# One gate tile moved from the indexer into the top-k selection, more matmul work a selection round, and a second buffer for the keys read back from DRAM

## The chip, the cores and the metric

The kernel runs on one core of a Trainium2 chip. The metric is the device time of one execution in microseconds (us), lower is better. Engines: PE is TensorE, which does all matrix products and transposes; DVE is VectorE; ACT is ScalarE; POOL is GpSimd; SP is SyncE, which here only issues DMA transfers. Each engine runs its own queue of instructions in order. An instruction that has to wait holds up all that is queued behind it.

## The reference

One inference step of one layer of a streaming encoder: a prompt of 1024 rows and a sample of 32 rows (T = 1024, TS = 32, NT = 1056 rows in all) with D_MODEL = 1024. What the change touches is this part (shapes for the prompt):

```
z = h @ w_in                    # columns: u, zs, q, k, v, za, qi, ki, wi, gm
logits = einsum('bthd,bsd->bths', qi, ki_all) * IDX_DIM ** -0.5   # 8 indexer heads of 64
score = einsum('bth,bths->bts', wi, relu(logits))                 # (1024, 1024), causal by chunks
top_val, top_idx = lax.top_k(score, n_sel)                        # 256 keys for a query, 136 for the sample
s = einsum('bthd,btkhd->bthk', q, kg) * HEAD_DIM ** -0.5          # attention over the chosen keys
merged = sigmoid(g_s) * (ys @ w_ps) + sigmoid(g_a) * (ya @ w_pa)  # g_s, g_a = the 2048 columns gm
```

The 2048 columns gm make 16 gate tiles of 128 columns. A gate tile is a product of h with 128 columns of w_in, a tanh, and a store to DRAM. It needs nothing but h and is read only much later, in the merge, so it may be done at any time before.

## The kernel before, in words

**Numbers.** Every matrix product with w_in is made of three passes in split fp32: weights wh + wl and activations hH + hL, `mm3` (L270), whose three matmuls stand on L271, L272 and L273. `wparts` (L253) makes wh (a rounded copy, L259 on ACT or L263 on POOL) and wl (a subtraction, L264 on DVE or POOL) of a raw tile of weights that L250 loads by DMA.

**The stream.** All products with w_in are jobs of a queue `Z` (class `Stream`, L574), each 128 output columns wide. A job has 8 steps over the contraction for each of three blocks of 256, 384 and 416 rows (`BW`), one `mm3` a step: 72 matmuls. Near its start, a job lets the next job's weights be split and those of the one after it be loaded (`ahead`, L600). At the end of a block, a function of the job takes the result out of PSUM: for a gate tile a tanh on ACT (`tg`, L707), and after the third block the store thD on SP (L709). The program doesn't run the queue in one go: `run(us)` (L652) emits steps worth so many us, by a cost written into the code (0.02 + 0.00132 times the block's rows a step: 0.36, 0.53 and 0.57 us, 11.6 us for a job). PE's order is the order in which the program is written (`manual_schedule`, L715), so these calls set what stands where on PE. In the selection and attention, DVE and ACT have the written order too (L1600); elsewhere, and on POOL and SP everywhere here, a scheduler chooses it.

**The indexer** (L1178 to L1235). The four indexer query tiles qi0 to qi3, two heads each, are stream jobs. For each pair of heads there is a loop over seven row tiles (`i` = 2 to 8; 8 is the sample) and two heads: two passes of products into `pss` (L1220, L1221), relu on ACT (`rl`, L1223), weighting and accumulation in the score tile on DVE (`sco`, L1226, L1228). After every such item, `run(0.25 + nk * FI)` puts a step of stream work on PE. `pss` and `rl` have two buffers each. The first products need `kiL`, which POOL makes (L77). Which jobs can be taken is set by `NI`:

```
Z.add(qijob(1), *(gate_job(f, se, ve) for f in range(NS, NI - 1)))            # L1135
Z.add(qijob(2), qijob(3), gate_job(NI - 1, se, ve), hold=True)                # L1136
```

With NS = 6 and NI = 8, gate tile 6 comes behind qi1 and is taken before and during the first pair's loop; qi2 fills the second pair's loop, qi3 the third's, gate tile 7 the fourth's. ACT and DVE split these tiles' weights (`se, ve`).

**The selection** (L1605 to L1661) finds the threshold of the 256th (136th) score of each row bit by bit in 32 rounds. A round counts, for seven score tiles, the keys that pass the trial threshold: four tiles on ACT (L1556), three on DVE (L1558, 1024, 896 and 640 keys). Then DVE compares the counts (`keep`, L1614) and makes the next threshold (`thr`, L1621), for which the counts of the next round wait. Between the counts and `keep` stands `run(RS)`: stream work of RS = 4.1 us a round. Whatever this emits for ACT or DVE (the blocks' way out of PSUM) thus stands at that place of their queues. The way out is emitted `LAG` = 4.5 us of stream cost after its block. After the rounds, `mark` (L1623) makes the masks `mb` for the seven tiles, mainly on DVE, with `run` calls worth 45 us of stream cost. Stream jobs here: K, V and Q of the first pair of attention heads, gate tiles 8 to 15 and the four tiles za0 to za3; POOL splits the weights (for za1 to za3, ACT makes wh). All jobs must have been emitted before attention begins (`Z.until("za3")`, L1663). While the selection runs, PSUM holds six blocks of stream results: two tiles with two blocks each (`pss`) and two with one (`pz`).

**The keys' way through DRAM.** The K job's result `zf` is stored (L1337), and read back by head into both halves of a tile `kd` of 128 x 512 (`khead`, L1273; two DMAs a load, L1281; two loads a head), from which DVE makes `kH` (L76) and DVE or POOL `kL` (L77). The cached keys `ckt` (L1342), which PE transposes (L1348), use the same buffer: tag "kd", one buffer.

**Attention** (L1689) has 4 x 17 items, each with products (`pss`, L1392), row minima of the negated scores with the mask added (L1398), exponentials (L1405), a transpose two items later (`turn`, L1485) and the product with the values three items later (`pspo`, L1502, L1504), with stream work between: the next pair's K, V, Q and later the products `m0` to `m7`. The merge and the output product follow.

## Time and profile before

| | us |
|---|---|
| median of 3 runs (1029.61 to 1031.7) | 1030.85 |
| the profiled execution | 1031.07 |
| its span, first to last instruction | 1029.3 |
| up to the indexer's first product | 308.5 |
| indexer, to the first K matmul of the selection | 79.0 |
| selection, to the last mask | 196.8 |
| attention, about to 870 | 285.7 |
| merge and output | 159.3 |

An instruction's row in the trace gives start, duration, engine, line, operation, result and operands, and in brackets the idle time before it and what ended it. Durations of matmuls overlap, since they are pipelined; their pace is read from the starts. The row of a stretch gives busy time and the number of instructions of each engine, then the clock granted to TensorE as a share of full speed.

### The profile page before, as it was taken

Reading aid. Unit: us, or ns where it says so; the run is one execution under the profiler, and the core shown is the slowest. Engines: PE = TensorE matmul, PEld = TensorE weight load, DVE = VectorE, ACT = ScalarE, POOL = GpSimd, SP = SyncE. Lnnn points to the kernel's source line nnn. Section 1 sums busy time; section 2 is a strip of 40 time slices with the busy share of each in tenths; the row PEclk is TensorE's granted clock in tenths of the full one; section 3 lists DMA queues with packets and bytes.
Section 4 is the critical chain, followed back from the end, with each engine's and each line's share of the span. In section 5 each row is a group of like instructions: output and inputs, shape, how many; then the busy total and the mean of one; then the engine's idle time right before and its main releaser. Section 6 shows DMA issues by size and latency. Waiting matters only on the chain.

```text
span 1029.3 us, 16904 instructions
## 1 busy us (share of the span) xinstructions
PE 974.4 (95%) x6034; PEld 904.5 (88%) x6034; DVE 762.7 (74%) x1743; ACT 526.5 (51%) x1126; POOL 233.4 (23%) x443
## 2 busy tenths in 40 slices
PE   5999999999999999989998999999999998999997
PEld 3789999999998889889998999999997997998786
DVE  4669899993866879899999758657557685886543
ACT  3642234435546666867994366466465554343111
POOL 3102400000010043333315423334311222530000
PEclk9999999999999999989998999999999999999999
DMA  9922524548483122323313422222416424653411
GB/s 318 277 78 84 147 74 120 128 98 260 134 260 103 40 83 83 93 65 106 102 63 105 136 85 63 88 79 63 132 56 205 131 64 151 209 171 118 133 62 61
DMA packets 134399, 124.24 MB, mean 121 GB/s; under 512 B 20400, under 2 KB 115076, under 8 KB 134316
## 3 DMA queue, kind: packets, MB, share of 16 engines
q1 hardware_dynamic: 133376, 122.62, 38.9%
q8 instruction: 47, 0.77, 0.3%
q10 hardware_dynamic: 780, 0.52, 0.2%
q14 instruction: 36, 0.29, 0.1%
q0 software_dynamic: 160, 0.03, 0.0%
HBM read 87.74 MB, written 34.83 MB: 119 GB/s over the span
## 4 chain that ended last, share of the span: by engine, by line
PE 70%; ACT 9%; DVE 8%; DMA 6%; issue 5%; POOL 1%; SPq 1%; POOLq 0%; ACTq 0%; DVEq 0%
PE pz L271 12%; PE pz L272 11%; PE pz L273 11%; ACT junkb L1556 5%; PE pss L1392 3%; PE psm L1891 3%; PE psm L1892 3%; PE psm L1893 3%; DMA wm<-in_w_mod 2%; PE pt L1485 2%; DVE junk L1558 2%; PE pspo L1504 2%; PE pss L271 2%; PE pss L273 2%; PE pss L272 2%
## 5 line engine op out<-in xcount | busy, mean ns | idle before, releaser
L271 PE MATMUL pz<-hH,wh 128*128 128x384 f32 (+4 forms) x760 | 259.9, 342 | 0.8 <-ACT tg L707 0.5
L272 PE MATMUL pz<-hL,wh 128*128 128x384 f32 (+4 forms) x760 | 250.4, 329 | 0.0
L273 PE MATMUL pz<-hH,wl 128*128 128x384 f32 (+4 forms) x760 | 250.3, 329 | 0.0
L264 POOL TENSOR_TENSOR wl<-raw,wh 128x256 fp32r<-128x256 f32 (+1 forms) x180 | 134.5, 777 | 105.5 <-ACT wh L259 105.2
L271 PEld LDWEIGHTS pz<-hH,wh 128*128 128x128 f32 (+1 forms) x760 | 143.1, 188 | 7.1 <-issue 3.0
L272 PEld LDWEIGHTS pz<-hL,wh 128*128 128x128 f32 (+1 forms) x760 | 142.5, 187 | 1.7
L273 PEld LDWEIGHTS pz<-hH,wl 128*128 128x128 f32 (+1 forms) x760 | 142.1, 187 | 1.3
L1556 ACT ACTIVATE junkb<-sco,thr 128x768 bf16<-128x768 f32 (+3 forms) x128 | 96.7, 756 | 32.0 <-DVE thr L1621 21.2
L1558 DVE TENSOR_SCALAR_CACHE_REDUCE junk<-sco,thr 128x1024 bf16<-128x1024 f32 (+2 forms) x96 | 105.4, 1098 | 2.2
L271 PE MATMUL pss<-hH,wh 128*128 128x256 f32 (+2 forms) x288 | 94.9, 329 | 7.7 <-POOL wl L264 4.1
L273 PE MATMUL pss<-hH,wl 128*128 128x256 f32 (+2 forms) x288 | 92.5, 321 | 2.4 <-POOL wl L264 2.4
L272 PE MATMUL pss<-hL,wh 128*128 128x256 f32 (+2 forms) x288 | 92.5, 321 | 0.0
L1488 DVE TENSOR_TENSOR PL<-pt,PH 128x512 fp32r<-128x512 f32 (+2 forms) x96 | 50.4, 552 | 34.4 <-ACT PH L1487 34.2
L263 POOL CAST wh<-raw 128x256 fp32r<-128x256 f32 x88 | 34.9, 437 | 175.7 <-PE pz L272 157.1
L271 PEld LDWEIGHTS pss<-hH,wh 128*128 128x128 f32 x288 | 57.3, 199 | 11.8 <-POOL wl L264 4.4
L1487 ACT CAST PH<-pt 128x512 fp32r<-128x512 f32 (+2 forms) x96 | 43.0, 483 | 46.4 <-PE pt L1485 45.2
L273 PEld LDWEIGHTS pss<-hH,wl 128*128 128x128 f32 x288 | 57.1, 198 | 3.1 <-POOL wl L264 3.1
L1228 DVE SCALAR_TENSOR_TENSOR sco<-rl,wi,sco 128x384 f32<-128x384 f32 (+6 forms) x49 | 46.9, 964 | 15.0 <-ACT rl L1223 13.9
L272 PEld LDWEIGHTS pss<-hL,wh 128*128 128x128 f32 x288 | 57.2, 199 | 0.3 <-DVE hL L77 0.2
L1223 ACT ACTIVATE rl<-pss 128x384 f32<-128x384 f32 (+6 forms) x56 | 40.9, 739 | 28.0 <-PE pss L1221 22.2
L1405 ACT ACTIVATE Sm<-Sm,mx 128x128 f32<-128x128 f32 (+8 forms) x68 | 52.7, 775 | 4.8 <-DVE mx L1398 4.4
L1893 PE MATMUL psm<-o,mL 128*128 128x512 f32 (+1 forms) x136 | 51.8, 381 | 0.0
(400 smaller groups left out, 2173.9 us busy)
## 6 DMA issues: line engine op xcount, KB each, us to landing
raw<-in_w_in SPq DMA_DIRECT2D x44, 512.0 KB
thD<-tg SPq DMA_DIRECT2D x16, 528.0 KB
tgl<-thD SPq DMA_DIRECT2D x16, 528.0 KB
wm<-in_w_mod SPq DMA_DIRECT2D x8, 1024.0 KB
rraw<-in_w_mod SPq DMA_DIRECT2D x4, 1024.0 KB
kd<-kd SPq DMA_DIRECT2D x32, 128.0 KB
xo<-in_x_prompt SPq DMA_DIRECT2D x8, 512.0 KB
rawo<-in_w_o SPq DMA_DIRECT2D x8, 512.0 KB
```

Of the source, the lines that this page charges most:

```text
L264: leng.tensor_sub(wl[:, c], raw[:, c], f32(wh[:, c]))
L271: te.matmul(ps, wh, xh, start=first, stop=False)
L272: te.matmul(ps, wh, xl, start=False, stop=False)
L273: te.matmul(ps, wl, xh, start=False, stop=last)
L1223: se.activation(rl[:m, :nk].rearrange("p (b c) -> p b c", c=w_), pv, AF.Relu)
L1228: ve.scalar_tensor_tensor(sco[i][:m, :nk], rl[:m, :nk], w, sco[i][:m, :nk], op0=ALU.mult, op1=ALU.add)
L1405: se.activation(P, P, AF.Exp, scale=-1.0, bias=self.mx, accum_out=self.rs)
L1487: se.copy(PH[:, b0:b1_, oc], src)
L1488: ve.tensor_sub(PL[:, b0:b1_, oc], src, f32(PH[:, b0:b1_, oc]))
L1556: se.activation(junkb[:m, :nk], x[:m], AF.Sign, bias=t, accum_out=cnt[:m, k:k + 1])
L1558: ve.tensor_scalar(junk[:m, :nk], x[:m], t, None, op0=ALU.is_lt, op1=ALU.add, accum_out=cnt[:m, k:k + 1])
L1893: te.matmul(ps, ml, wh, start=False, stop=last)
```

## The change

Three numbers of the code are changed, and two places use the last of them:

```diff
-NS, NI = 6, 8
+NS, NI = 6, 7
-LAG, RS, MS, RM, RB = 4.5, 4.1, 0.008, 14.0, 1
+LAG, RS, MS, RM, RB = 4.5, 4.6, 0.008, 14.0, 1
         def load(b):
             c = slice(512 * b, 512 * b + 512)
-            kd = ap_.tile([128, 512], F32, name="kd", bufs=1)
+            kd = ap_.tile([128, 512], F32, name="kd", bufs=2)
             for hf_ in range(2):
                 sp.dma_start(kd[64 * hf_:64 * hf_ + 64], X.kd[64 * e:64 * e + 64, c])
...
             def fin_():
-                ckt = ap_.tile([128, 4, 128], F32, name="ckt", tag="kd", bufs=1)
+                ckt = ap_.tile([128, 4, 128], F32, name="ckt", tag="kd", bufs=2)
```

With NI = 7 the list on L1135 holds no gate tile, and gate tile 6 takes the place of tile 7 on L1136. Tile 7 becomes the first of nine gate tiles in the selection, `gate_job(f, ge, ge) for f in range(NI, 16)` (L1571), and POOL splits its weights. RS = 4.6 puts 32 x 0.5 = 16 us more of stream cost into the 32 rounds.

On PE, the queue loses the gate tile's matmuls before and inside the first pair's loop. Before, the loop's start (`pss` are the indexer's products, `pz` the gate tile's):

```order
L1220 MATMUL pss<-kiH,qis_2929 128x384
L1221 MATMUL pss<-kiL,qis_2929 128x384
L271 MATMUL pz<-hH_738,wh 128x416
L272 MATMUL pz<-hL_739,wh 128x416
L273 MATMUL pz<-hH_738,wl 128x416
L1220 MATMUL pss<-kiH,qis_2930 128x384
L1221 MATMUL pss<-kiL,qis_2930 128x384
```

and with the change, from the transposes ahead of the loop (`pg` is a small product for the output gate):

```order
L1185 MATMUL pt<-idf,cki 128x128 x4
L1194 MATMUL pt<-idf,zki 128x72 x8
L1194 MATMUL pt<-idf,zki 32x72
L1167 MATMUL pg<-rraw,scP 32x512 x4
L1220 MATMUL pss<-kiH,qis_2929 128x384
L1221 MATMUL pss<-kiL,qis_2929 128x384
L1220 MATMUL pss<-kiH,qis_2930 128x384
L1221 MATMUL pss<-kiL,qis_2930 128x384
```

The 72 matmuls of one job are gone from there, 24 of them from inside the loop, and stand in the selection.

On ACT, the blocks leave PSUM earlier, counted in rounds. At the end of the rounds (L1556 are the counts of one round, `tg` a gate block, `wh` the weights of za1, L1629 the first instruction of the marks) before:

```order
L707 ACTIVATE tg<-pss 128x384
L259 CAST wh<-raw 128x1024
L1629 ACTIVATE junkb,cnt<-le 128x1024
L707 ACTIVATE tg<-pz 128x416
L696 ACTIVATE zt<-pss 128x256
```

and with the change, where `wh` stands a round earlier and the last gate block and the first block of za0 (`zt`) ahead of the marks:

```order
L259 CAST wh<-raw 128x1024
L1556 ACTIVATE junkb,cnt<-sco_3313,thr 128x768
L1556 ACTIVATE junkb,cnt<-sco_3311,thr 128x512
L1556 ACTIVATE junkb,cnt<-sco_3310,thr 128x384
L1556 ACTIVATE junkb,cnt<-sco_3316,thr 32x544
L707 ACTIVATE tg<-pz 128x416
L696 ACTIVATE zt<-pss 128x256
L1629 ACTIVATE junkb,cnt<-le 128x1024
```

Before, the 24 gate blocks of the selection leave from round 10 on (rounds counted from 0); with the change, 27 of them from round 9 on.

On SP, the reads of the keys move. In the selection, from the store of the first K result on, before:

```order
L1337 DMA kd_4423<-zf 128x1024
L1267 DMA out_k_p<-tm 128x8x128
L250 DMA raw<-in_w_in 128x8x128
L1268 DMA out_k_s<-tm 32x128
L1281 DMA kd<-kd_4423 64x512 x2
L1267 DMA out_v_p<-tm 128x8x128
L250 DMA raw<-in_w_in 128x8x128
```

and with the change:

```order
L1337 DMA kd_4337<-zf 128x1024
L1281 DMA kd<-kd_4337 64x512 x2
L1267 DMA out_k_p<-tm 128x8x128
L1268 DMA out_k_s<-tm 32x128
L250 DMA raw<-in_w_in 128x8x128
L1281 DMA kd<-kd_4337 64x512 x2
L1267 DMA out_v_p<-tm 128x8x128
```

The first read stands right behind the store, and a load of weights (L250) has moved behind one more store.

## The prediction

> **What bounds the kernel now.** I read the page first, then stretches of the span, then who waits for whom in the two stages that the change touches, and last single rows. On the page, the busy time of the engines and their share of the span:
>
> ```profile
> PE 974.4 (95%) x6034; PEld 904.5 (88%) x6034; DVE 762.7 (74%) x1743; ACT 526.5 (51%) x1126; POOL 233.4 (23%) x443
> ```
>
> PE is short of 100% by 55 us. The change takes no matmul away, so it can only gain from this idle time and from time at a lower clock. Where these lie, the stretches show: the rounds up to the attention heads' last keys, the rest of the rounds, and the marks. The columns are length, busy time (instructions) of PE, PEld, DVE, ACT and POOL, and the granted clock.
>
> ```profile
> 396.30:450.60 54.30, 52.09 (x326) 50.26 (x324) 48.17 (x104) 41.59 (x101) 17.22 (x34) 1.00 0.29 84
> 450.60:541.90 91.30, 84.10 (x505) 82.25 (x504) 85.14 (x196) 79.02 (x191) 26.00 (x48) 0.96 0.28 88
> 541.90:584.30 42.40, 39.10 (x226) 38.34 (x227) 40.70 (x58) 17.03 (x39) 20.93 (x23) 0.92 0.35 114
> ```
>
> Here DVE is as full as PE. The pace is that of the rounds, as the rows of `thr` show, which end a round each (start, duration):
>
> ```profile
> 404.88 0.17 DVE L1621 SCALAR_TENSOR_TENSOR thr<-keep,nxt 128x7 int32<-128x7 int32 x1
> 408.87 0.17 DVE L1621 SCALAR_TENSOR_TENSOR thr<-keep,nxt 128x7 int32<-128x7 int32 x1
> 413.04 0.67 DVE L1621 SCALAR_TENSOR_TENSOR thr<-keep,nxt 128x7 int32<-128x7 int32 x1
> 444.51 0.17 DVE L1621 SCALAR_TENSOR_TENSOR thr<-keep,nxt 128x7 int32<-128x7 int32 x1
> 496.20 0.66 DVE L1621 SCALAR_TENSOR_TENSOR thr<-keep,nxt 128x7 int32<-128x7 int32 x1
> 541.73 0.17 DVE L1621 SCALAR_TENSOR_TENSOR thr<-keep,nxt 128x7 int32<-128x7 int32 x1
> ```
>
> A bare round takes 408.87 - 404.88 = 3.99 us. The last eleven take (541.73 - 496.20) / 11 = 4.14. The rounds with the heads' extra work are longer: from 413.04 (round 4) to 444.51 (round 9) five take 31.5 us. PE waits for these rounds, because a block's way out of PSUM stands on ACT behind them:
>
> ```profile
> PE pss L271 <- POOL wl L264: 4.1, 1, 4.1
> PE pss L273 <- POOL wl L264: 2.4, 2, 1.7
> PE pt L1261 <- ACT tm L1263: 2.2, 2, 2.0
> PE pss L271 <- ACT tg L707: 1.6, 2, 0.8
> PE pss L271 <- ACT wh L259: 1.2, 1, 1.2
> PE pss L271 <- POOL wh L263: 0.7, 1, 0.7
> PE pz L271 <- ACT tg L707: 0.5, 1, 0.5
> ```
>
> This is PE from 387 to 585 us, in all 12.7 us. The longest wait is put down to POOL, but just before it ended ACT took the block of 384 columns out of the `pss` tile that PE needed, behind the counts of round 11; its row and that of the wait follow. What the wait cost beyond its 4.05 us, two stretches of one block each show (24 matmuls of 256 columns):
>
> ```profile
> 454.09 0.46 ACT L707 ACTIVATE tg<-pss 128x384 f32<-128x384 f32 x1
> ```
> ```profile
> 454.69 0.55 PE L271 MATMUL pss<-hH,wh 128*128 128x256 f32 x1 [4.05 <-POOL wl L264]
> ```
> ```profile
> 411.51:414.23 2.72, 2.72 (x25) 2.72 (x24) 2.50 (x7) 2.24 (x7) 2.68 (x6) 1.00 0.03 9
> 454.69:459.95 5.26, 5.26 (x24) 5.26 (x25) 5.02 (x15) 3.87 (x10) 0.01 (x1) 0.50 0.05 18
> ```
>
> After the wait the clock is 0.50, and the block takes 5.26 us instead of 2.72. So the selection is bound by DVE's and ACT's rounds, and PE stands idle at their side; and a wait of 4 us on PE costs 2.5 more behind it.
>
> **The change part by part.** *The indexer loses a job.* One stream job is 72 matmuls; one such stretch, then the rows at the first pair's loop (POOL makes `kiL`; PE's first product; PE's first stream matmul behind the loop), the loop's stretch, and the relus in it (ACT alone):
>
> ```profile
> 438.93:450.50 11.57, 11.57 (x73) 11.34 (x72) 10.37 (x21) 4.59 (x11) 4.44 (x9) 1.00 0.18 47
> ```
> ```profile
> 304.07 3.56 POOL L77 TENSOR_TENSOR kiL<-kid,kiH 128x1568 fp32r<-128x1568 f32 x1 [12.71 <-DVE kiH L76]
> 308.50 0.34 PE L1220 MATMUL pss<-kiH,qis 128*128 128x384 f32 x1
> 323.63 0.33 PE L271 MATMUL pz<-hH,wh 128*128 128x384 f32 x1
> ```
> ```profile
> 308.50:323.60 15.10, 13.80 (x73) 12.07 (x73) 9.61 (x13) 11.06 (x16) 0.00 (x0) 1.00 0.41 137
> ```
> ```profile
> 308.50:323.60 15.10, 9.43 (x13) 1.00 0.41 137
> ```
>
> So 11.57 us of PE work leave this place, but not 11.57 us of time. The first product can't start before `kiL` is there, at 304.07 + 3.56 = 307.6 instead of 308.5. The loop is then bound by its 14 relus, 14 x 9.43 / 13 = 10.2 us, with about 0.5 of a first product ahead: 10.7 us at full clock. But PE will have been idle for most of 300 to 307.6, and as after the wait at 454.69 I expect half clock for some 5.3 us, which costs 2.6 us of PE work; the relus hide a part, I take 2.0. PE leaves the loop at 307.6 + 12.7 = 320.3 instead of 323.6: **3.3 us earlier**. The bounds: full clock all along, 5.3 earlier; half clock all along, where PE's own work in the loop (15.1 less 1.3 idle, less the gate tile's block of 416 of 1056 columns, 4.6, so 9.2) doubles to 18.5, which is 2.5 later. Behind it nothing changes: gate tile 6 fills the fourth loop as tile 7 did, so the 3.3 us arrive at the selection.
>
> *The selection gains a job.* First DVE's side. Its work up to the last mask is the same, less a wait for the keys:
>
> ```profile
> DVE kH L76 <- DMA kd<-kd: 1.0, 1, 1.0
> ```
>
> The second buffer lets this read start early: -1.0 us. Against it stands POOL, which now splits tile 7: in the row of 413.04 `thr` took 0.67 instead of 0.17 beside POOL's work; `keep` and the next `nxt` stand at the same place, so one more job costs up to 3 x 0.5 = 1.5, and I take 1.0, so that the two cancel. Three more blocks on ACT in the rounds lie in the 0.15 us that 4.14 exceeds 3.99 by. The last mask:
>
> ```profile
> 583.86 0.43 DVE L1637 TENSOR_TENSOR mb<-le,eq 32x544 bf16<-32x544 bf16 x1
> 586.14 0.31 DVE L1414 TENSOR_SCALAR Sm<-Sm,rs 128x128 f32<-128x128 f32 x1
> ```
>
> It ends at 584.3 now, so at 581.0, and the first attention item is ready for its transpose 2.2 us later, at 583.2.
>
> A rule of the Trainium skill speaks against this part: "SBUF — State Buffer", section "Who interferes with whom", says that VectorE and GpSimd share a pair of ports under an exclusive lock, and that the loser waits for a whole instruction. The row of 413.04 agrees in kind. Taken at its worst, DVE would stand for the whole 4.4 us of POOL's work on a job (an estimate, from the stretch of 438.93); the masks would then end 3.4 us later than I say, the transpose would be ready at 586.6 and not 584.9 (below), and the time would be 1.7 us longer, 1026.6.
>
> *PE's side.* From the first K matmul to the first attention product, and the first transpose of attention:
>
> ```profile
> 387.55 0.38 PE L271 MATMUL pss<-hH,wh 128*128 128x256 f32 x1
> 583.18 0.22 PE L1392 MATMUL pss<-kH,qs 128*128 128x128 f32 x1
> 589.91 0.27 PE L1485 MATMUL pt<-idf,Sm 128*128 128x128 f32 x1
> ```
>
> 583.18 - 387.55 = 195.6 us. Off go 12.7 of waits, 2.6 at half clock (0.5 x 5.26) and 8% of the 42.4 us of the marks at clock 0.92, 3.4: 176.9 of work. With one job more it is 188.5. With RS = 4.6 a round holds 4.6 x 11.57 / 11.6 = 4.6 us of PE work, so blocks leave PSUM in earlier rounds (order on ACT above), and the waits for them shrink. I keep the 2.2 for `tm`, which the slow rounds cause, and of the other 10.5 about 2.3 (the weights of za1 still pass ACT, then POOL), with 1.0 at half clock. So 384.25 + 188.5 + 5.5 = 578.2 us for the end of the stream. PE then has 589.91 - 583.18 = 6.7 us to do ahead of the first transpose, which needs no mask: 584.9, later than DVE's 583.2. The first transpose stands at 584.9 instead of 589.9: **5.0 us earlier**. The bounds: if half of the 10.5 and half of the 6.0 lost to the clock stay, the stream ends at 384.25 + 188.5 + 2.2 + 5.3 + 3.0 = 583.2 as now, and nothing is gained here; if all go, DVE's 583.2 sets the transpose, 6.7 earlier.
>
> *Attention.* PE waits here for the cached keys, twice:
>
> ```profile
> PE pt L1348 <- DMA ckt<-in_cache_k: 2.6, 2, 1.7
> ```
>
> With its own buffer `ckt` can be read before the last keys are used. But on SP, the reads now wait right behind the store of the keys, and weights behind them; those have 10 us to spare now. Between 0 and 2.6 us I take 1.0.
>
> The sum is 5.0 + 1.0 = 6.0 us off the profiled 1031.07, which is 0.2 above the median of 1030.85; so off the median too: **1024.9 us**. One measurement tells about 0.2% (2.1 us) from no change.
>
> **The rivals.** *PE stays at half clock through the first pair's loop.* Speaking for it: the loop starts after some 7 us of little work, and its waits for the relus break it up. Against: at full clock such waits did not lower it (1.00 in the stretch of 308.50). The loop ends 2.5 us later than now, PE's stream at 390.05 + 188.5 + 5.5 = 584.0, 0.8 later than now, less 1.0 in attention: 1030.7. The Trainium skill has a rule for this, in "TensorE: Matmul & The Clock Gate", Part 1, "What's actually happening": half rate after an idle window of about 3.4 us, full rate only after about 3.4 us of sustained work. By that rule the loop gets warm if its first products are dense, and not if the relus thin them out; the 0.50 behind 454.69 agrees with the rule.
>
> *The rounds wait for PE* (slower). With 4.6 us of matmuls in a round of 4.14, PE falls back by 0.46 a round, in the 22 rounds from 10 to 31 by 10 us. Once its lead is gone, ACT stands before each `tg`, and behind it the next round's counts. All of it would put the masks at 591, 6.7 later than now, less 1.0: 1036.6. It decides when PE's lead at the end of round 9 is used up: by the rows, PE has then done ten rounds' work, 384.25 + 46 + 2 of transposes = 432, and `thr` comes at 444.5 - 3.3 = 441.2. The lead of 9 and the lag of 4.5 that the code leaves a block cover the 10 us. It takes a lead under 5.5 at that point.
>
> *All goes well:* full clock in the loop (2.0 more), no waits but `tm`'s (DVE then sets 581.2 for the transpose), all 2.6 in attention: 8.7 + 2.6 = 11.3 us, 1019.6.
>
> **How the numbers follow.** My forecast has 0.58 (1022 to 1028), the cold loop 0.16, the rounds that wait for PE 0.12, all well 0.14. The range of 1021.0 to 1031.0 leaves out the slower rival and half of the last. Faster by over 0.2%: 0.58 + 0.14 + 0.03 of the cold loop, 0.75; within 0.2%: the other 0.13 of the cold loop and 0.01 of the slower rival, 0.14; slower 0.11.
>
> **What would show it.** Right: the first K matmul at about 384 instead of 387.6; no wait of 4 us on PE in the rounds, and clock 1.00 there; the last mask near 581, the first transpose of attention near 585; no wait of PE for `ckt`. Wrong: a low clock from 308 to 324 with the first K matmul at 388 or later; `thr` rows 4.6 apart, with ACT waiting for PE before `tg`; or a new wait of POOL for weights that SP loads late.

## The result, and the profile after

| | before | with the change |
|---|---|---|
| median | 1030.23 us (4 runs, 1029.58 to 1031.7) | 1018.31 us (4 runs, 1018.0 to 1018.76) |
| the profiled execution | 1031.07 | 1018.76 |
| its span | 1029.3 | 1017.0 |

The ratio is 0.9883, with a 95% interval of 0.9866 to 0.9900: 11.9 us faster, about twice the 6.0 us that were forecast, and below the range. From the page of the changed kernel, the line of the busy times; PE has the same 6034 matmuls to do, so the time came out of its idle time and its clock:

```profile
PE 968.4 (95%) x6034; PEld 900.7 (89%) x6034; DVE 762.5 (75%) x1742; ACT 525.7 (52%) x1125; POOL 241.2 (24%) x451
```

**The head.** The profiled execution of the changed kernel started badly, with a low clock (last column but two) where before, in the same stretch and with the same order on PE, had full clock. First before, then after:

```profile
15.00:30.00 15.00, 13.77 (x82) 8.73 (x74) 8.63 (x35) 6.85 (x13) 5.21 (x10) 1.00 1.09 355
```
```profile
15.00:30.00 15.00, 13.03 (x86) 9.15 (x87) 9.15 (x36) 7.45 (x14) 5.70 (x10) 0.67 1.09 354
```

The last matmul of qi1's stream (the end of the head) thus stands at 301.7 us instead of 299.3, 2.4 us later, which is none of the change's doing. So all that follows is measured from a point of the same kernel, not from zero.

**The indexer.** In the changed kernel, POOL's `kiL`; the small product `pg` and PE's wait for its weights; the first product; the first stream matmul behind the loop; the first K matmul:

```profile
306.18 3.50 POOL L77 TENSOR_TENSOR kiL<-kid,kiH 128x1568 fp32r<-128x1568 f32 x1 [12.40 <-DVE kiH L76]
308.31 1.94 PE L1167 MATMUL pg<-rraw,scP 128*32 128x512 f32 x8 [3.46 <-DMA rraw<-in_w_mod]
310.18 0.69 PE L1220 MATMUL pss<-kiH,qis 128*128 128x384 f32 x1
323.05 0.33 PE L271 MATMUL pz<-hH,wh 128*128 128x384 f32 x1
384.27 0.36 PE L271 MATMUL pss<-hH,wh 128*128 128x256 f32 x1
```

The loop takes 323.05 - 310.18 = 12.87 us, where it took 323.63 - 308.50 = 15.13. Two stretches of before, then of after, from the end of qi1's stream to the end of the first loop and from there to the first K matmul, and of after the whole of the low clock there:

```profile
299.29:323.63 24.34, 23.04 (x143) 20.15 (x140) 15.69 (x19) 14.76 (x24) 3.56 (x1) 1.00 0.60 180
323.63:387.55 63.92, 60.70 (x338) 53.73 (x336) 49.37 (x63) 38.48 (x60) 11.95 (x15) 0.97 0.19 59
```
```profile
301.72:323.05 21.33, 15.23 (x70) 9.52 (x68) 12.04 (x18) 12.74 (x20) 3.50 (x1) 0.84 0.50 152
323.05:384.27 61.22, 59.18 (x339) 52.34 (x337) 48.81 (x62) 38.62 (x60) 12.07 (x15) 1.00 0.19 61
```
```profile
306.83:313.66 6.83, 5.35 (x16) 2.49 (x16) 1.04 (x3) 1.58 (x3) 2.84 (x1) 0.50 0.83 231
```

24.34 became 21.33, 3.0 us less; and 63.92 became 61.22, another 2.7 less, in a part where the forecast had seen no change.

**The selection.** Stretches of the changed kernel: rounds 1 to 10, rounds 11 to 31, the marks. Then who PE waits for from the first K matmul on, and three rows at the end (the last mask; the first attention product; the first transpose of attention):

```profile
393.40:450.20 56.80, 56.33 (x362) 55.52 (x361) 49.88 (x106) 41.90 (x102) 22.87 (x41) 1.00 0.31 90
450.20:541.20 91.00, 88.10 (x544) 86.81 (x543) 85.02 (x195) 80.70 (x195) 28.26 (x52) 1.00 0.30 95
541.20:584.00 42.80, 40.56 (x257) 39.94 (x257) 41.21 (x58) 16.58 (x37) 23.33 (x24) 1.00 0.38 126
```
```profile
PE pz L271 <- ACT tg L707: 2.0, 1, 2.0
PE pss L1392 <- ACT zt L696: 1.6, 1, 1.6
PE pss L271 <- ACT tg L707: 0.8, 1, 0.8
PE pz L271 <- ACT zt L696: 0.6, 1, 0.6
PE pt L1261 <- ACT kall L1349: 0.5, 1, 0.5
PE pt L1485 <- DVE Sm L1414: 0.4, 1, 0.4
```
```profile
583.53 0.43 DVE L1637 TENSOR_TENSOR mb<-le,eq 32x544 bf16<-32x544 bf16 x1
577.23 0.33 PE L1392 MATMUL pss<-kH,qs 128*128 128x128 f32 x1 [1.63 <-ACT zt L696]
585.50 0.33 PE L1485 MATMUL pt<-idf,Sm 128*128 128x128 f32 x1 [0.45 <-DVE Sm L1414]
```

PE's waits fell from 12.7 us to 5.9, and the clock is 1.00 all along. But DVE's side did not move up with the indexer: from the first K matmul to the end of the last mask it took 196.7 us and takes 583.96 - 384.27 = 199.7. Its first ten rounds grew most (56.80, before 54.30). The first transpose now waits for DVE (`Sm`).

**Attention and behind.** From the first transpose of attention to its last product with the values, before and after, and what PE waits for there most in the changed kernel:

```profile
589.90:867.80 277.90, 267.32 (x1784) 250.10 (x1783) 185.64 (x536) 160.85 (x371) 80.85 (x173) 0.99 0.31 97
```
```profile
585.50:857.50 272.00, 265.07 (x1783) 249.51 (x1784) 186.93 (x539) 161.28 (x372) 81.06 (x173) 1.00 0.32 100
```
```profile
PE pz L271 <- DVE m L1590: 2.3, 2, 1.5
PE pspo L1504 <- DVE PL L1488: 0.8, 1, 0.8
PE pt L1485 <- ACT Sm L1412: 0.8, 2, 0.5
```

No wait for `ckt` is left. The 12.3 us between the spans are then: head -2.4, indexer 5.7 (88.26 less 82.55), from the first K matmul to the first transpose 1.1 (202.36 less 201.23), attention 5.9, and what follows it 2.0 (161.5 less 159.5).

### The profile page after: what moved, and what is told of

The parts are those of the page before. It is cut to its first block, busy times and chain, and to the rows that moved or that the text cites. A ratio compares the mean times of both kernels' runs of the same rounds, so it can differ in the third digit from the quotient of the medians.

```text
span 1017.0 us, 16923 instructions
## 1 busy us (share of the span) xinstructions
PE 968.4 (95%) x6034; PEld 900.7 (89%) x6034; DVE 762.5 (75%) x1742; ACT 525.7 (52%) x1125; POOL 241.2 (24%) x451
## 4 chain that ended last, share of the span: by engine, by line
PE 66%; DVE 12%; ACT 12%; DMA 5%; issue 4%; SPq 1%; POOLq 0%; POOL 0%; ACTq 0%; DVEq 0%
PE pz L271 11%; PE pz L272 11%; PE pz L273 10%; ACT junkb L1556 7%; PE pss L1392 3%; PE psm L1891 3%; PE psm L1892 3%; PE psm L1893 3%; DVE junk L1558 3%; PE pt L1485 2%; DMA wm<-in_w_mod 2%; PE pspo L1504 2%; PE pspo L1502 2%; PE pss L1220 2%; PE psm L273 2%
## 5 line engine op out<-in xcount | busy, mean ns | idle before, releaser
L271 PE MATMUL pz<-hH,wh 128*128 128x384 f32 (+4 forms) x744 | 254.0, 341 | 2.9 <-ACT tg L707 2.0
L272 PE MATMUL pz<-hL,wh 128*128 128x384 f32 (+4 forms) x744 | 245.0, 329 | 0.0
L273 PE MATMUL pz<-hH,wl 128*128 128x384 f32 (+4 forms) x744 | 244.8, 329 | 0.0
L264 POOL TENSOR_TENSOR wl<-raw,wh 128x256 fp32r<-128x256 f32 (+1 forms) x184 | 137.9, 779 | 101.1 <-ACT wh L259 100.8
L271 PEld LDWEIGHTS pz<-hH,wh 128*128 128x128 f32 (+1 forms) x744 | 139.6, 188 | 7.6 <-ACT tg L707 2.3
L272 PEld LDWEIGHTS pz<-hL,wh 128*128 128x128 f32 (+1 forms) x744 | 138.9, 187 | 1.6
L273 PEld LDWEIGHTS pz<-hH,wl 128*128 128x128 f32 (+1 forms) x744 | 138.6, 186 | 1.3
L1556 ACT ACTIVATE junkb<-sco,thr 128x768 bf16<-128x768 f32 (+3 forms) x128 | 96.7, 756 | 31.8 <-DVE thr L1621 21.5
L272 PE MATMUL pss<-hL,wh 128*128 128x256 f32 (+2 forms) x304 | 95.7, 315 | 0.0
L273 PE MATMUL pss<-hH,wl 128*128 128x256 f32 (+2 forms) x304 | 95.3, 313 | 0.0
L263 POOL CAST wh<-raw 128x256 fp32r<-128x256 f32 x92 | 39.2, 466 | 168.9 <-PE pz L272 152.6
L1228 DVE SCALAR_TENSOR_TENSOR sco<-rl,wi,sco 128x384 f32<-128x384 f32 (+6 forms) x49 | 46.8, 960 | 12.9 <-ACT rl L1223 11.9
```

What stands on the lines that cost most here:

```text
L264: leng.tensor_sub(wl[:, c], raw[:, c], f32(wh[:, c]))
L271: te.matmul(ps, wh, xh, start=first, stop=False)
L272: te.matmul(ps, wh, xl, start=False, stop=False)
L273: te.matmul(ps, wl, xh, start=False, stop=last)
L1228: ve.scalar_tensor_tensor(sco[i][:m, :nk], rl[:m, :nk], w, sco[i][:m, :nk], op0=ALU.mult, op1=ALU.add)
L1556: se.activation(junkb[:m, :nk], x[:m], AF.Sign, bias=t, accum_out=cnt[:m, k:k + 1])
```

## The experiments

The theory to begin with: each part earns in its own stage, tile and share in the indexer and the selection, the buffers in attention. The rival: attention's gain comes from the schedule. The table has every run; the ratio is that to the kernel before, with its interval. "Loop" goes from the indexer's first product to the first stream matmul behind the first loop, "rest" from there to the first K matmul; "masks" and "transpose" from the first K matmul to the last mask's end and the first transpose of attention; "attention" from there to the last product with the values (us, from each kernel's profile).

| | ratio | loop | rest | masks | transpose | attention |
|---|---|---|---|---|---|---|
| before | 1 | 15.13 | 63.92 | 196.7 | 202.4 | 277.9 |
| the change | 0.9883 (0.9866 to 0.9900) | 12.87 | 61.22 | 199.7 | 201.2 | 272.0 |
| e1 buffers alone | 0.9958 (0.9943 to 0.9974) | 15.12 | 63.89 | 195.9 | 201.8 | 275.8 |
| e2 tile and share | 0.9920 (0.9899 to 0.9941) | 12.86 | 61.18 | 199.4 | 200.9 | 277.6 |
| e3 tile alone | 0.9999 (0.9983 to 1.0015) | 13.17 | 61.18 | 195.7 | 206.6 | 278.9 |
| e4 share alone | 0.9961 (0.9949 to 0.9973) | 15.12 | 62.40 | 197.1 | 198.6 | 277.5 |
| e5 change, share late | 0.9965 (0.9951 to 0.9980) | 12.46 | 61.18 | 199.6 | 204.1 | 278.9 |
| e6 change, ckt's own buffer | 0.9878 (0.9857 to 0.9899) | 12.82 | 61.19 | 199.7 | 201.2 | 275.8 |
| e7 change, PE kept busy | 0.9880 (0.9861 to 0.9900) | 12.01 | 61.21 | 199.6 | 201.1 | 272.5 |
| e8 change, pg later | 0.9914 (0.9894 to 0.9933) | 17.99 | 63.02 | 198.9 | 200.5 | 272.4 |
| e9 change, old order in attention | 0.9898 (0.9881 to 0.9915) | 12.44 | 61.20 | 200.2 | 201.7 | 275.0 |
| e10 change, a third order | 0.9883 (0.9864 to 0.9902) | 13.29 | 61.24 | 199.0 | 200.6 | 274.5 |
| e11 before, new order in attention | 0.9964 (0.9951 to 0.9977) | 15.12 | 62.41 | 196.4 | 201.9 | 275.5 |
| e12 change, keys early | 0.9905 (0.9888 to 0.9921) | 18.50 | 61.34 | 200.1 | 201.6 | 273.1 |
| e13 buffers and new order | 0.9939 (0.9923 to 0.9955) | 15.13 | 62.39 | 196.2 | 201.0 | 273.1 |
| e14 change, keys early, PE busy | 0.9866 (0.9848 to 0.9884) | 12.44 | 61.43 | 200.1 | 201.7 | 272.2 |

### The parts of the change alone

The buffers (e1):

```diff
-            kd = ap_.tile([128, 512], F32, name="kd", bufs=1)
+            kd = ap_.tile([128, 512], F32, name="kd", bufs=2)
-                ckt = ap_.tile([128, 4, 128], F32, name="ckt", tag="kd", bufs=1)
+                ckt = ap_.tile([128, 4, 128], F32, name="ckt", tag="kd", bufs=2)
```

> The kernel before with the second buffer for the returning keys alone (NI = 8, RS = 4.1). Theory A, each part of the change earns in its own stage: the reads of the cached keys, which PE waited for twice (2.6 us in all), start early, and since PE is the bound in attention all of it arrives, with what the clock loses behind such a wait; 3 to 5 us faster than before, no wait of PE for ckt, and nothing gained ahead of 590 us. Theory B, what attention gained in the changed kernel comes from the schedule (an emptier or other order of the stream) and the reads were late for their place in SP's queue: 0 to 1 us faster, with the wait for ckt only moved.

Tile and share (e2), the tile alone (e3), the share alone (e4):

```diff
-NS, NI = 6, 8
+NS, NI = 6, 7
-LAG, RS, MS, RM, RB = 4.5, 4.1, 0.008, 14.0, 1
+LAG, RS, MS, RM, RB = 4.5, 4.6, 0.008, 14.0, 1
```

> The kernel before with NI = 7 and RS = 4.6 together, one buffer for the returning keys. Theory A: the indexer and the selection give 5 to 8 us, the first transpose of attention stands 5 to 7 us earlier, and both waits for ckt stay in attention; 5 to 8 us faster than before, and together with the kernel that has the buffers alone the 11.9 us of the whole change. Theory B: 10 to 12 us faster, without the buffers.

> The kernel before with NI = 7 alone: the gate tile goes into the selection, but a round still takes RS = 4.1. Theory A, the larger share is what lets the selection's idle PE take the job: without it the tile's 11.6 us come behind the last mask, since the rounds hold no more stream work than before, the indexer's 5 to 6 us are lost again, and the whole is 2 to 7 us slower than before. Theory B, the rounds' pace is set by DVE and the share matters little: 3 to 6 us faster than before.

> The kernel before with RS = 4.6 alone, the gate tile still in the first pair's loop of the indexer. Theory A: the waits in the rounds (12.7 us) shrink, PE is done with its jobs ahead of the last mask and then waits for it, so that DVE sets the start of attention: 0 to 3.5 us faster than before, the first K matmul at 387.5 as before. Theory B, the gain of the whole change lies in the larger share: 5 to 8 us faster.

The ratios of e1 and e2 multiply to 0.9878, the whole change's 0.9883: theory A holds for the parts. The buffers give 4.3 us (0.42% of 1029.72; 2.7 to 5.9 by the interval). PE's order is that of before to the last instruction, and the lead over before is flat (0.3 us) until the first wait for `ckt` is missing; it is 1.4 behind that, and 3.3 behind the second. So two waits of 0.91 and 1.67 us cost 1.14 and 1.85: more than their idle time.

Tile and share need each other. The tile alone gains nothing: the indexer's gain is there, but the stream comes 4 us later than the masks and the first transpose stands at 206.6 instead of 202.4. The share alone frees PE far ahead of the masks, as the rows of e4 show, the first attention product and the first transpose:

```profile
567.67 0.22 PE L1392 MATMUL pss<-kH,qs 128*128 128x128 f32 x1
586.78 0.47 PE L1485 MATMUL pt<-idf,Sm 128*128 128x128 f32 x1 [10.23 <-DVE Sm L1414]
```

PE is there 15.5 us earlier than before (583.18), and waits 10.2 for the mask. One job of 11.6 us fits into that, nearly to the brim. Behind this wait the clock is at 0.50 from 580.97 to 591.21. For e4, theory A's figure (0 to 3.5 us faster) comes near the 4.0 measured; for e3 neither theory's time came (2 to 7 us slower or 3 to 6 faster; there is no difference), but the mechanism of theory A shows in its rows. The times of these runs are not tile and share alone: e2 and e4 also have the changed kernel's order of the stream in attention, and e3 has a third one (below). By e11 the changed kernel's order alone is worth 3.7 us, so the 4.0 of e4 don't show that the larger share earns anything by itself.

### Where the larger share belongs

The changed kernel with the larger share from round 10 on only (e5):

```diff
-        run(RS)
+        run(RS if b < 22 else 4.1)
```

> The changed kernel, but the larger share of stream work (RS = 4.6) only from round 10 on; rounds 0 to 9 take 4.1 as before. In the changed kernel the time from the first K matmul to the last mask grew from 196.7 to 199.7 us, and rounds 6 to 10 (418.02 to 450.43 before, 415.48 to 450.04 after) from 32.4 to 34.6. Theory A, the larger share brings the first pair of heads' work on DVE and ACT into fewer rounds, earlier, and they grow by it: rounds 6 to 10 fall back to about 32.4, the last mask stands about 2 us earlier behind the first K matmul, PE then sets the first transpose of attention, 0.5 us or so earlier; 0 to 1 us faster than the changed kernel (ratio to before 0.987 to 0.988). Theory B, the job that POOL splits more costs DVE the time by waits at their shared way to memory: rounds 6 to 10 stay at 34.6 and the masks too.

Rounds 6 to 10 did fall back, from 34.6 us (415.48 to 450.04) to 32.3 (415.14 to 447.46): there theory A is right. It earned nothing, though: the masks stand where they stood (199.6), and the kernel is about 8 us slower than the changed one. Rounds 11 to 31 took 93.5 us instead of 91.0, for the work went there: the split of the returning keys on DVE (`kH`, `kL`) takes 4.9 us in them, in the changed kernel 2.7. Their stretch in e5:

```profile
447.60:541.10 93.50, 89.91 (x554) 89.10 (x553) 88.30 (x197) 79.92 (x194) 30.78 (x56) 0.98 0.29 95
```

The rows of `thr` in the rounds, grouped (busy us, mean ns of one), of before, after and e5:

```profile
L1621 DVE SCALAR_TENSOR_TENSOR thr<-keep,nxt 128x7 int32<-128x7 int32 x31 | 7.4, 238 | 1.2 <-DVE keep L1614 0.2
```
```profile
L1621 DVE SCALAR_TENSOR_TENSOR thr<-keep,nxt 128x7 int32<-128x7 int32 x31 | 8.1, 261 | 1.2 <-DVE keep L1614 0.2
```
```profile
L1621 DVE SCALAR_TENSOR_TENSOR thr<-keep,nxt 128x7 int32<-128x7 int32 x31 | 9.2, 297 | 1.2 <-DVE keep L1614 0.2
```

With `nxt` and `keep`, which behave alike, it is 21.5 us before, 22.7 after, 25.1 in e5. How much POOL does in the rounds is not the measure (busy for 43.2 us before, 51.1 after, 48.6 in e5), but how many of these short operations meet one of its instructions: in the sixteen profiles of this case 1071 of them have no instruction of POOL beside them and take 0.14 to 0.17 us, and of the 417 that have one, 322 take over 0.3. So theory B has its part too. And PE, with less to do in the early rounds, comes to the marks late: the first transpose at 204.1. Of the 9.9 us between the spans of this kernel and the changed one (1026.9 and 1017.0), 6.8 lie in attention. e5 has an order of its own there, as the next point shows; what that order costs was not run by itself.

### The order of the stream in attention

What `run` has left over when attention begins (its credit) decides after which item a step of the stream falls, in all of attention. The change of RS alone shifts it: 0.178 before and in e1, 0.239 after and in e2 and e4; 0.359 in e3, 0.069 in e5 (worked out from the code). PE's order before (-) and after (+) at one such place:

```
+L271 MATMUL pz<-hH,wh 128x256
+L272 MATMUL pz<-hL,wh 128x256
+L273 MATMUL pz<-hH,wl 128x256
 L1392 MATMUL pss<-kH,qs 128x448
 L1392 MATMUL pss<-kL,qs 128x448
 L1392 MATMUL pss<-kH,qs 128x448
 L1392 MATMUL pss<-kL,qs 128x448
 L271 MATMUL pz<-hH,wh 128x256
 L272 MATMUL pz<-hL,wh 128x256
 L273 MATMUL pz<-hH,wl 128x256
-L271 MATMUL pz<-hH,wh 128x256
-L272 MATMUL pz<-hL,wh 128x256
-L273 MATMUL pz<-hH,wl 128x256
 L1261 MATMUL pt<-idf,zf 128x128
```

One step has gone ahead of an item, as at about a dozen places.

Three runs set the credit by hand, behind `Z.flush()` and before attention begins: the changed kernel with the old value (e9, shown) or with that of e3 (e10), the kernel before with the new one, 0.23868 (e11).

```diff
-    Z.lag = 0
+    Z.lag, Z.credit = 0, 0.17768
```

> The changed kernel, but the stream's credit (what run has left over when attention begins) is set to 0.178, its value in the kernel before, instead of the 0.239 that the larger share leaves; PE's order in attention is then that of the kernel before, instruction by instruction. Theory A, the step at which the stream's work falls between the items of attention matters: from the first transpose of attention to the last product with the values the changed kernel takes 272.0 us and the kernel before with the buffers alone 275.8; this one takes about 275.8, the waits for Sm (1.9 us in 4) and m (2.9 in 3) of the kernel before come back, and it is 2.5 to 4 us slower than the changed kernel (ratio to before 0.991 to 0.992). Theory B, the order in attention is of no weight, and the 3.7 us are luck of the executions: as fast as the changed kernel (0.988).

> The changed kernel with the stream's credit at the start of attention at 0.359, the value that the tile alone had left. Theory A: another order again, attention takes 272 to 277 us, where a kernel with the same order but one buffer took 278.9, 3.3 of it one wait for the cached keys; 0 to 4 us slower than the changed kernel. Theory B: as fast as the changed kernel.

> The kernel before with nothing but the stream's credit at the start of attention set to 0.239, as the changed kernel has it; PE's order ahead of attention is that of before and in attention that of the changed kernel. Theory A: the order is worth 2 to 4 us by itself, less what the waits for the cached keys (one buffer still) take back: from the first transpose to the last product with the values 274 to 277.6 us instead of 277.9, 0.3 to 4 us faster than before. Theory B: no difference (0 to 0.5 us).

And one, before with the buffers and the new order, and nothing else (e13):

> The kernel before with the two buffers and the stream's credit of 0.239 at the start of attention, and nothing else: no tile moved, no larger share. Theory A, buffers and order give attention's gain together, whatever happens ahead of it: from the first transpose of attention to the last product with the values 272 to 273 us, instead of 277.9 in the kernel before, and the whole 5 to 7 us faster than before (ratio 0.993 to 0.995). Theory B, they only gain together with an earlier start of attention: 275 us or more, 2 to 4.5 us faster.

The attention stretches of e9, e11 and e13:

```profile
582.50:857.50 275.00, 266.02 (x1784) 249.60 (x1785) 186.25 (x539) 161.04 (x372) 80.93 (x173) 1.00 0.32 98
```
```profile
589.50:865.00 275.50, 265.81 (x1785) 249.29 (x1784) 186.70 (x536) 161.07 (x371) 80.76 (x173) 1.00 0.32 98
```
```profile
587.10:860.20 273.10, 265.43 (x1785) 249.42 (x1784) 186.32 (x536) 160.93 (x371) 80.56 (x173) 1.00 0.33 99
```

Three pairs differ in this order alone: after and e9 (272.0 and 275.0), e13 and e1 (273.1 and 275.8), e11 and before (275.5 and 277.9). It is worth 2.4 to 3.0 us of attention in each. That is one profile against one, and part of it belongs to the executions: the clock is at 0.50 for 3.4 us from 784.35 on in before and for 6.8 us from 781.02 on in e1, and not in e11 or e13; and e9 waits 1.1 us longer for `ysLD` than the changed kernel. With the old order the waits for `Sm` and `m` are 1.9 and 2.9 us, in e9 as before; with the new one 0.8 and 2.3. In the times the order alone is shown by e11 (0.9964, 3.7 us of 1030.38, 2.4 to 5.0 by the interval); between after and e9 and between e1 and e13 the intervals overlap. This is theory A for e11 and e13 (0.9939); for e9 the loss of 1.5 us (0.9898 against 0.9883) is less than the 2.5 to 4 of theory A. e10's order costs 2.4 us of attention in the profile and none in the times, which this pair does not settle.

So the buffers and a shift that is no part of the change's text make about half of its gain (0.9939, 6.3 us). For tile and share 0.9883 / 0.9939 = 0.9944 is left, 5.8 us.

### Which buffer

The changed kernel with one buffer for `kd` and one of its own for `ckt` (e6):

```diff
-            kd = ap_.tile([128, 512], F32, name="kd", bufs=2)
+            kd = ap_.tile([128, 512], F32, name="kd", bufs=1)
-                ckt = ap_.tile([128, 4, 128], F32, name="ckt", tag="kd", bufs=2)
+                ckt = ap_.tile([128, 4, 128], F32, name="ckt", tag="ckt", bufs=1)
```

> The changed kernel with one buffer for the returning keys again and a buffer of its own for the cached keys, so as many buffers as the change has, otherwise divided. Theory A, only the cached keys' wait for a shared buffer cost anything: as fast as the changed kernel (ratio to before 0.987 to 0.990), no wait of PE for ckt, and DVE's wait of 1.0 us for the first kd back, which costs nothing. Theory B, the early reads of kd earned part of it: 1.5 to 4 us slower than the changed kernel.

0.9878 against 0.9883: as fast as the change, theory A. What cost time was that the cached keys had to wait for a buffer that the keys on their way back from DRAM still held. The 275.8 of its profile come from one wait, 3.7 us with the clock behind it, for a transfer that the other profiles do not show in this length; the profiled execution was the slowest of its five (1020.9, the others 1016.6 to 1018.2):

```profile
785.83 0.71 PE L272 MATMUL pz<-b,wh 128*128 128x416 f32 x1 [1.81 <-DMA b<-ysLD]
```

### The clock at the first loop

In e7, 16 transposes of the identity stand ahead of `pg`:

```diff
-            for k in range(4):
-                te.matmul(pg[32 * k:32 * k + 32, :], scP[:, 4 * k4 + k], raw[:, k], start=k4 == 0, stop=k4 == 1)
+            for k in range(0 if i else -16, 4):
+                te.transpose(pg[:, :128], idf, idf) if k < 0 else te.matmul(pg[32 * k:32 * k + 32, :], scP[:, 4 * k4 + k], raw[:, k], start=k4 == 0, stop=k4 == 1)
```

In e8 `pg` stands later:

```diff
-        Z.after(RM, mm)
+        Z.after(RM - 1 if i else RM + 4, mm)
-            Z.after(RM + 1, lambda: rpiece(i + 1, c))
+            Z.after(RM if i else RM + 5, lambda: rpiece(i + 1, c))
```

In e12 and e14 the keys are split in two, the first part ahead of `run(KF)`, with DVE in the written order there; e12 also loads `pg`'s weights ahead of the keys, e14 loads them ahead of the biases and has transposes as in e7, 14 ahead of the token transposes and 20 ahead of `pg`:

```diff
-    split(kiH, kiL, kid, ve, ge)
+    split(kiH[:, 0:1024], kiL[:, 0:1024], kid[:, 0:1024], ve, ge)
...
+    split(kiH[:, 1024:1568], kiL[:, 1024:1568], kid[:, 1024:1568], ve, ge)
```

> The changed kernel with 16 more transposes of the identity on PE, put ahead of the small product of the output gate (pg) that PE waits for by 3.4 us before the first pair's loop; their result is overwritten, so the output is the same. Theory A, the half clock from 306 to 311 us is the price of that idle time, and a busy PE keeps the clock up: pg takes 1.0 instead of 1.9 us, the first products of the loop come at full clock, and the first K matmul stands 1 to 2 us earlier behind the end of qi1's stream. Theory B, ACT's relus bound the loop and hide the half clock: pg shorter, the loop's end unmoved (0 to 0.4 us).

> The changed kernel with the first of the four small products of the output gate (pg) 4 us of stream cost later, behind the loop's third row tile, and the other three 3 to 4 us later as well. Theory A, pg's wait for its weights (3.4 us) and its 1.9 us at half clock set the loop's start beside POOL's kiL: the first product then starts when kiL is there, 0.2 to 0.5 us earlier, not more, since kiL ends only 0.4 us ahead of it; the loop then holds pg instead, and the first K matmul moves by -0.5 to +0.5 us. Theory B, pg is what the loop waits for: 1 to 2 us earlier.

> A try for a faster version: the changed kernel with the first load of the output gate's weights ahead of the keys' loads, and the indexer keys split in two pieces (1024 keys first), DVE's cast of the first ahead of the queries' last blocks. Theory A, the start of the first pair's loop is now set by kiL (ready 8.3 us behind the end of qi1's stream) and by pg's weights beside it: both come earlier, the first product stands 2 to 3 us earlier behind qi1's stream, the first K matmul 1.5 to 3 us, and since DVE's and ACT's rounds follow the first K matmul it arrives at the end: 1.5 to 3 us faster than the changed kernel (ratio to before 0.985 to 0.987). Theory B, the loop's relus and a half clock for longer give it back: 0 to 0.5 us.

> The changed kernel with an earlier start of the first pair's loop and a PE kept busy ahead of it: the keys split in two pieces (1024 first, right behind their load), the output gate's weights loaded ahead of its biases, and 34 transposes of the identity in PE's idle time (14 ahead of the token transposes, 20 ahead of pg; their results are overwritten). Theory A, the half clock is what made the two earlier starts worse: with a busy PE the first product comes 1 to 2 us earlier behind the end of qi1's stream than in the changed kernel (8.8 us), at full clock, and the first K matmul stands 79.5 to 81.5 us behind it instead of 82.9; 1 to 3 us faster than the changed kernel (ratio to before 0.985 to 0.987). Theory B, the loop itself doesn't profit from an earlier start, since the relus and the next weights set it: the first K matmul at 82 us or later.

The loop's stretch in e7, e12 and e14, one line each:

```profile
308.99:320.95 11.96, 10.48 (x52) 7.49 (x49) 8.45 (x12) 8.99 (x13) 0.00 (x0) 1.00 0.26 88
```
```profile
305.94:324.40 18.46, 14.47 (x51) 10.73 (x49) 14.55 (x21) 9.43 (x13) 5.63 (x2) 0.64 0.38 114
```
```profile
307.04:319.44 12.40, 10.69 (x52) 7.42 (x49) 9.95 (x16) 9.28 (x13) 1.36 (x1) 1.00 0.42 132
```

Two rows of e7, the transposes and `pg`, and two of e12, DVE's cast of the first keys and the product that waited for `kiL`:

```profile
304.48 3.58 PE L1167 MATMUL pg<-idf 128*128 128x128 f32 x16 [0.42 <-ACT wtok L1196]
308.00 1.06 PE L1167 MATMUL pg<-rraw,scP 128*32 128x512 f32 x8
```
```profile
305.19 0.69 DVE L76 CAST kiH<-kid 128x1024 fp32r<-128x1024 f32 x1 [9.86 <-DMA kid<-zki]
309.27 0.69 PE L1225 MATMUL pss<-kiL,qis 128*128 128x384 f32 x1 [2.65 <-POOL kiL L77]
```

With PE busy, `pg` takes 1.06 us instead of 1.94 and the loop 12.0 instead of 12.9 at full clock; the first K matmul stands 81.6 us behind the start of qi1's last matmul instead of 82.9. That is theory A, at its lower end. It is not more than executions differ by: with the changed kernel's code up to there, e9 and e10 have 81.6 and 84.0 in their profiles, with the clock at 0.50 for 3.4 and 10.2 us. In the times (0.9880 and 0.9883) it does not show. In e12 the first product came 2 us earlier, and the second stood 2.65 us for `kiL`: DVE had waited for the load of the keys until 305.19, behind that of `pg`'s weights. With such gaps among its first products the loop ran at half clock for its first 13.2 us and took 18.5; in e8, with a wait of 2.88 us at the same product, it took 18.0. For e8 and e12 both theories were wrong: the early start did not gain little, it cost 4 us at the first K matmul. e14 has the same early keys and a busy PE: clock 1.00, no wait for `kiL`, loop 12.4. Of the 6 us between the two loops 2.65 are that wait, which e14 avoids by loading the keys ahead of `pg`'s weights; the rest goes with the clock, which no run changed alone here. The early start itself brings little once the clock is right (81.8 us in the count of above, between the two theories and no better than e7). e14 is the fastest kernel of the study, 1016.13 us where the change has 1018.31; between the two the intervals overlap.

The rule of the Trainium skill that the prediction named for this rival ("TensorE: Matmul & The Clock Gate", Part 1, "What's actually happening": full rate only after about 3.4 us of sustained work) agrees with e7, where the clock is 0.50 from 304.43 to 307.84, during the transposes, and 1.00 behind them, and with e12, where it is 0.50 from 302.10 to 319.16 and rises only behind the first 3.41 us in which PE is busy all the time (from 315.75 on). Its other half, half rate after an idle window of about 3.4 us, is too narrow for this case: a wait of 1.49 us was enough in before (last section).

## Why the prediction was wrong in size

Direction and most of the mechanism were right; the sum was half of what came. The forecast had 3.3 us for the indexer, 1.7 for the selection (5.0 less 3.3), 1.0 for attention and nothing behind it. The spans have 5.7, 1.1, 5.9 and 2.0, and 2.4 lost in the head.

**The indexer's loop: right, its size with luck.** 3.3 us forecast, 3.0 measured; half clock for 6.8 us (5.3 forecast), and a loop of 12.9 where 12.7 had been said. Two errors cancel in that: at full clock the loop takes 12.0 (e7) and not 10.7, and the half clock, taken as 2.0, costs 0.9 in the loop (1.3 with `pg`), for only 3.5 of the 6.8 us lie in it. Why the loop is not at 10.7 stays open. That PE would wait for `pg`'s weights was not foreseen; it cost 0.5 us at most, since `kiL` ended only that much ahead of the first product. The cold loop was a real danger: e12 took its bound of 18.5 us, though 2.65 of that are a wait that the bound doesn't hold. That the first K matmul stands at 384.27, where 384.25 was forecast, is luck as well: the head's loss makes up for what the next point gained.

**"Behind it nothing changes": wrong by 2.7.** 1.2 of it is real: with 62.4 in e4, e11 and e13, which have the order of before here, and 61.2 in the changed one, the second loop starts 0.5 us sooner behind the first stream matmul, and a wait in it is 1.07 us instead of 1.49. The other 1.5 belongs to the profiled execution of before (see the last section).

**DVE's side: wrong, against the change.** The forecast let the wait for `kd` (1.0 less) and POOL's splitting (1.0 more) cancel. Both came about as said, 0.85 less in e1's masks and 22.7 - 21.5 = 1.2 more; the 4.4 us of the worst case did not come. What was missed is that the larger share brings the first heads' work into rounds 6 to 10, which grew by 2.2 us. Another 0.7 lies ahead of that: from the first K matmul to the end of round 1 it takes 13.7 us where it took 13.0, as in e3 with the tile alone. The masks came at 199.7 instead of the 196.75 forecast. It is only partly explained: in e4 these rounds grew as much (34.6), but its marks gave it back (41.3 instead of 42.6), so that the masks are 2.7 to 3.0 us later with tile and share together and 0.4 at most with either.

**PE's side: right, but it was not what set the transpose.** The stream's end was to stand 193.95 us behind the first K matmul, PE was at the first attention product 192.96 behind it; the transpose 200.65, and it is 201.2, behind a wait of 0.45 for DVE's late `Sm`. PE's waits are 5.9 us (4.5 forecast), and no clock is lost. The rival in which rounds wait for PE did not come: the rows show PE waiting for ACT, at no time the rounds for PE.

**Attention: the term that failed.** "Between 0 and 2.6 us I take 1.0" was 5.9, and 2.0 more behind attention. The bound of 2.6 was too low, since a wait costs more than its idle time: 3.0 for the two in e1. And the step left out the order: that RS changes the credit with which attention begins, and so the place of every later step, could be read from the code and from PE's order behind the marks; it is worth another 2.4 to 3.0 in these profiles. Of the 2.0 behind attention, some 1.1 are there in e1, e11 and e13 as well (160.3 to 160.5 instead of 161.5), with a wait of 0.5 us in the merge gone; what makes the rest was not tried.

## What to carry to other kernels

Where a program interleaves two kinds of work by a running balance, every change of a share also moves all that comes after: compare the order to the end of the program, not only near the change, and try a few starting balances for themselves. A wait of 1 to 2 us on a nearly full TensorE cost a little more than its idle time here, and nearly twice that where the clock dropped behind it. An engine's idle time can take in a job only if the rounds let its results out earlier: moving the job alone, or the share alone, was worth 0 and 4 us, both together 8. These figures include the shift of the order; without it, 5.8 are left for both together (0.9944) and next to nothing for the share alone (0.9961 against e11's 0.9964), within the intervals.

## What the runs showed of the hardware

The same wait in the same program lowers the clock in some executions and not in others. Before the last items of the second loop PE waits 1.49 us for a relu, in before and e1 as in e4, e11 and e13. Its row in before, and the stretch of 6.6 us around it in before and in e4:

```profile
342.87 0.31 PE L1220 MATMUL pss<-kiH,qis 128*32 128x272 f32 x1 [1.49 <-ACT rl L1223]
```
```profile
341.00:347.60 6.60, 4.88 (x20) 4.08 (x19) 6.32 (x8) 3.92 (x6) 0.00 (x0) 0.74 0.30 82
```
```profile
343.20:349.80 6.60, 4.88 (x29) 4.02 (x28) 6.31 (x8) 4.29 (x7) 0.00 (x0) 1.00 0.30 82
```

With the clock at 0.74, 20 matmuls pass instead of 29, and the rest of the indexer takes 63.9 us instead of 62.4: 1.5 us, in two of five executions.

Where the wait falls seems to decide it. In each of the sixteen profiles the stretches at 0.50 start whole multiples of 3.41 us apart and last 3.41, 6.83, 10.24, 13.65 or 17.07 us, but for the one that the end of the program cuts short. So the clock is set anew every 3.41 us, on a grid that lies differently in each execution. The stretch of the grid that holds the wait, and the next one, in before and in e4:

```profile
340.61:344.03 3.42, 1.70 (x10) 0.87 (x9) 3.34 (x5) 3.08 (x5) 0.00 (x0) 1.00 0.09 18
344.03:347.44 3.41, 3.41 (x14) 3.34 (x13) 3.20 (x4) 1.23 (x2) 0.00 (x0) 0.50 0.51 143
```
```profile
342.04:345.45 3.41, 1.92 (x10) 1.28 (x9) 2.98 (x4) 3.37 (x6) 0.00 (x0) 1.00 0.01 4
345.45:348.86 3.41, 3.17 (x21) 2.84 (x19) 3.27 (x4) 1.21 (x3) 0.00 (x0) 1.00 0.56 154
```

With 1.70 us of PE's work in such a stretch the clock falls in the next (in e1 1.69), with 1.91 to 2.07 (e13, e4, e11) it doesn't. Elsewhere the border is less sharp: before has 2.10 in the stretch ahead of the low clock at 784.35. No run moved the wait on purpose.

The second wait for `ckt` shows it as well; its row and the stretch around it, in e2 and in e11:

```profile
739.67 0.63 PE L1348 MATMUL pt<-idf,ckt 128*128 128x128 f32 x4 [1.98 <-DMA ckt<-in_cache_k]
```
```profile
738.00:743.00 5.00, 3.33 (x16) 3.31 (x17) 0.93 (x3) 1.76 (x4) 0.00 (x0) 0.76 0.35 103
```
```profile
746.45 0.63 PE L1348 MATMUL pt<-idf,ckt 128*128 128x128 f32 x4 [1.91 <-DMA ckt<-in_cache_k]
```
```profile
744.80:749.80 5.00, 3.35 (x22) 3.21 (x23) 1.42 (x5) 2.27 (x5) 0.00 (x0) 1.00 0.37 106
```

There the low clock cost 1.6 us more (the difference between the two kernels before and behind the wait); PE has 1.43 us of work in the stretch of the grid in e2 and 1.86 in e11. So the price of a wait has two values, and a single profile shows one of them: before's happened to hold the dear one in the indexer, after's a low clock from 15 to 45 us.
